# Attention scores as three 64-row products on alternating row halves, in a two-layer encoder of three head groups

## The chip, the core and the metric

The kernel runs on one core of a Trainium2 chip. The metric is the device time of one execution in microseconds. The core has a matrix engine (TensorE; the profile shows its products as PE and the loads of its stationary operands as PEld), VectorE (DVE), ScalarE (ACT), GpSimd (POOL) and a DMA queue that SyncE (SP) issues.

## The reference

Each of two layers normalises x (1024 tokens of 1024 numbers), projects it, and lets three groups of heads work on the result: an mLSTM group, an HGRN2 group and a differential-attention group. Their gated outputs are projected back and added to x. The change touches the attention group, which has four heads. Each head is a pair of query heads and a pair of key heads of 64 numbers, and one value head of 128:

```python
def differential_attention(q, k, v, lam, positions):
    q = rope_partial(q, positions) * (Dq ** -0.5)
    k = rope_partial(k, positions)
    def block(qi):                       # 128 queries against all 1024 keys
        s = jnp.einsum("bqnd,bknd->bnqk", qi, k).astype(jnp.float32)
        p = jax.nn.softmax(s, axis=-1).reshape(B, Hh, 2, Q_BLOCK, S)
        w = p[:, :, 0] - lam * p[:, :, 1]
        return jnp.einsum("bhqk,bkhv->bqhv", w.astype(v.dtype), v)
```

The rotary embedding turns the first 16 of the 64 numbers of a query or key.

## The kernel before

All arrays are float32. Where TensorE is to take a product fast, an operand a is split into a high part in the type fp32r (rounded by an ACT copy) and a low part (the rest, a DVE or GpSimd subtraction), and three products, high by high, high by low and low by high, are summed in PSUM. The input projections are made so (`proj_token`, line 308, and `proj_channel`, line 295: 24 products in one PSUM tile), and the output projection too (line 1058).

**The attention scores** use another form of the split. A head's 64 numbers fill half of the 128 rows of the array, so `evqk` (line 958) writes each 64-number head twice side by side, four heads of 2 x 64 for a tile of 128 tokens. `qk_half` (line 918) rotates both copies (lines 925 to 931) and transposes each doubled head, four tiles of 128 tokens to a PSUM tile (line 936): 16 transposes for 512 tokens. ACT copies the transposed head into fp32r (lines 938 and 941). For a query head, DVE then overwrites rows 64 to 127 with the rest (line 939), so that `Q1` holds the high part above the low part. For a key head all 128 rows are kept as `KH`, which is the high part twice, and `KL`, the low part twice (line 942). A product of `Q1` with `KH` over 128 rows is then high by high plus low by high, and one with `KL` the two other terms.

For each of the four heads (`hd`), each of eight tiles of 128 queries (`qt`) and both query heads of the pair (`n`), two halves of 512 keys (`kb`) take two products each (lines 991 and 992) into one PSUM tile of 1024 columns, `ps_s2`, of which there are two buffers. DVE takes the maximum (line 994) and scales it (995), ACT the exponential and its sum (998). Then the two heads' exponentials are combined on DVE (1003 to 1007), transposed on TensorE (1012), copied out of PSUM by ACT and DVE (1014 and 1016), multiplied with the values (1019), and squared and gated (1021 and 1022). `o_post` (line 901) normalises and transposes a finished head.

**What sets the order.** While head `hd` is worked on, the input projections of head `hd` + 1 are written into the same loop as a generator (`a_proj`, line 944), one piece for each query tile: two tiles of tokens, 48 products of 256 columns. Head 3 has no next head; there the output projection (line 1050 on), which follows in the program, is available. The instruction order on each engine isn't that of the text: the program is built with `schedule_with_timeline_sim=True`, by which a planner lets the program run in a simulation and gives each engine, whenever it is free there, the instruction that stands first in the text among those whose operands and buffers are ready. The order so found is fixed in the program, and each engine then works through it strictly.

Of the kernel before, what the change touches and what calls it, by code (L numbers as in the profile page):

```python
# [9 lines left out]
F32 = mybir.dt.float32  # L10
F32R = mybir.dt.float32r
I32 = mybir.dt.int32
U8 = mybir.dt.uint8
AF = mybir.ActivationFunctionType
ALU = mybir.AluOpType
AX = mybir.AxisListType

P = 128
D = 1024
S = 1024  # L20
# [10 lines left out]
QK = 64  # L31
DMIX = 2048
EPS = 1e-6
HALF = 8
# [56 lines left out]
def trunk(ctx, tc, x_in, positions, w_in, w_out, pvec, rvec, out, dbg=None):  # L91
    nc = tc.nc
# [10 lines left out]
    def ps_mx(name):  # L103
        return pp.tile([P, 512], F32, tag="mx", name=name)

    def ps_s2(name):
        return pp.tile([P, 1024], F32, tag="s2", name=name)
# [12 lines left out]
    ident = cp.tile([P, P], F32, name="ident")  # L120
# [226 lines left out]
    for l in range(DEPTH):  # L347
# [6 lines left out]
        mu_d = dr.tile([8, S], F32, name=f"mu_{l}")  # L354
        mpl_d = dr.tile([16, 8], F32, name=f"mpl_{l}")

        # ------------------------------------------------------------ input norm
        h = []
        if l:
            npool = ExitStack()  # L360
# [1 line left out]
        for half in range(2):  # L362
# [5 lines left out]
            for t4 in range(4):  # L368
                tt = half * 4 + t4
# [14 lines left out]
            for k in range(8):  # L384
                ps = ps_mx(f"hT{l}{half}{k}")
# [6 lines left out]
        npool.close()  # L392
        hpool = ExitStack()
        gp = hpool.enter_context(tc.tile_pool(name=f"hg{l}", bufs=1))
        # ------------------------------------------------------------ mLSTM: conv, q/k/v, gates
        mpool = ExitStack()
        m1 = mpool.enter_context(tc.tile_pool(name=f"mg{l}", bufs=1))
        G = []
        gates = m1.tile([P, NT, 16], F32, name=f"gates{l}")
        nc.vector.tensor_copy(gates, bgate[:, l].unsqueeze(1).broadcast_to([P, NT, 16]))  # L400
        with tc.tile_pool(name=f"ma{l}", bufs=2) as ma:
# [38 lines left out]
            for i in range(3):  # L440
                parts = load_win(l, ("xm", i)) if l or i else xm0
                for jj in range(2):
# [9 lines left out]
                    for k in (0, 1, 3, 4):  # L452
                        d = k - 2
# [8 lines left out]
                    for src, rhs, dd, nm in ((xc, WA[j], xct_d, "a"), (xm, BV[j], v_d, "v")):  # L462
                        tk = ma.tile([P, NT, P], F32, tag="tk", name=f"tk{nm}{l}{j}", bufs=1)
                        for t0 in range(0, NT, 4):
                            ps = ps_s2(f"tk{nm}{l}{j}{t0}")
# [29 lines left out]
        with tc.tile_pool(name=f"mb{l}", bufs=1) as mB:  # L495
# [27 lines left out]
            for d in range(2):  # L523
                rows = []
                for nm, src in (("i", igt), ("f", lgf)):
                    rt = mB.tile([4, S], F32, tag="gr" + nm, name=f"gr{nm}{l}{d}", bufs=2)
                    for half in range(2):
                        ps = ps_mx(f"gr{nm}{l}{d}{half}")
# [12 lines left out]
                for c in order:  # L541
                    sl = slice(c * P, (c + 1) * P)
# [10 lines left out]
                for i, (src, dst) in enumerate(((ir, a_tok), (br, b_tok), (mu, m_tok))):  # L553
                    ps = ps_mx(f"gt{l}{d}{i}")
# [13 lines left out]
                nc.scalar.activation(t, t, AF.Exp)  # L568
            nc.scalar.activation(flr, flr, AF.Exp, scale=-1.0)

        # ------------------------------------------------------------ mLSTM: chunk recurrence
        with tc.tile_pool(name=f"mc{l}", bufs=1) as mp:
            for hd in range(MH):
                pr_, hh_ = divmod(hd, 2)
# [12 lines left out]
                q = mp.tile([P, 2, S], F32, tag="m8", name=f"q{l}{hd}", bufs=2)  # L587
                for i, g in enumerate((G[jA], G[jC][:, hh_])):
                    for half in range(2):
                        sl = slice(half * 512, (half + 1) * 512)  # L590
                        ps = ps_mx(f"q{l}{hd}{i}{half}")
# [3 lines left out]
                for half in range(2):  # L595
                    ps = ps_mx(f"qk{l}{hd}{half}")
                    for c4 in range(4):
                        c = half * 4 + c4
                        sl = slice(c * P, (c + 1) * P)
# [21 lines left out]
                for i in range(NT):  # L621
                    for d in range(2):
                        c = i if d == 0 else NT - 1 - i
                        C = Cs[d]
                        sl = slice(c * P, (c + 1) * P)
                        pn = ps_mx(f"num{l}{hd}{d}{c}")
                        nc.tensor.matmul(pn[:, :MD + 1], W[(d, c)], vt[:, c], start=True, stop=True)
                        n = mp.tile([P, MD + 1], F32, name=f"n{l}{hd}{d}{c}", tag="n", bufs=2)
# [28 lines left out]
                nc.sync.dma_start(hs_d[hd], hsum)  # L657
        mpool.close()

        # ------------------------------------------------------------ HGRN2  # L660
        def slab(name, tag, bufs=None):
            return gp.tile([P, S], F32, tag=tag, name=f"{name}{l}", bufs=bufs or 1)

# [174 lines left out]
            nc.scalar.activation(yo, ps, AF.Copy, scale=hgs[:, l, hd:hd + 1])  # L838
            nc.sync.dma_start(yT[6 + hd], yo)

        # ------------------------------------------------------------ mLSTM: output gates
        md = hpool.enter_context(tc.tile_pool(name=f"md{l}", bufs=1))

        mo = {}
# [51 lines left out]
            {"i": hgrn_iz, "r": hgrn_rest, "o": mlstm_om, "z": mlstm_zm}[step[0]](int(step[1]))  # L896
        hpool.close()

        # ------------------------------------------------------------ attention
        with tc.tile_pool(name=f"at{l}", bufs=2) as ap, tc.tile_pool(name=f"aw{l}", bufs=1) as aw:  # L900
            def o_post(hd, gt, ss, r):
                rstd(ss, r, P)
# [10 lines left out]
                    nc.scalar.activation(yo[:, half * 512:(half + 1) * 512], ps, AF.Copy, scale=ags[:, l, hd:hd + 1])  # L913
                nc.sync.dma_start(yT[12 + hd], yo)

            sets = [ap.tile([P, 3, 2, S], F32R, name=f"qks{l}0", bufs=1), None]

            def qk_half(hd, half, qk):
                Q1, KH, KL = (sets[hd % 2][:, i] for i in range(3))
                cs = cosb[:, half * 4:half * 4 + 4].unsqueeze(2).broadcast_to([P, 4, 4, HALF])  # L920
                sn = sinb[:, half * 4:half * 4 + 4].unsqueeze(2).broadcast_to([P, 4, 4, HALF])
                x1 = qk[:, :, :, 0, 0:HALF]
                x2 = qk[:, :, :, 0, HALF:2 * HALF]
                tmp = [ap.tile([P, 4, 4, HALF], F32, tag=f"rt{i}", name=f"rt{i}{l}{hd}{half}", bufs=1) for i in range(4)]
                nc.vector.tensor_tensor(tmp[0], x1, cs, op=ALU.mult)
                nc.vector.tensor_tensor(tmp[1], x2, sn, op=ALU.mult)
                nc.vector.tensor_tensor(tmp[2], x2, cs, op=ALU.mult)
                nc.vector.tensor_tensor(tmp[3], x1, sn, op=ALU.mult)
                for dup in range(2):
                    nc.vector.tensor_sub(qk[:, :, :, dup, 0:HALF], tmp[0], tmp[1])  # L930
                    nc.vector.tensor_add(qk[:, :, :, dup, HALF:2 * HALF], tmp[2], tmp[3])
                sl = slice(half * 512, (half + 1) * 512)
                for n in range(4):
                    ps = ps_mx(f"qkT{l}{hd}{n}{half}")
                    for t in range(4):
                        nc.tensor.transpose(ps[:, t * P:(t + 1) * P], qk[:, t, n].rearrange("p a d -> p (a d)"), ident)
                    if n < 2:
                        nc.scalar.activation(Q1[:, n, sl], ps, AF.Copy)
                        nc.vector.tensor_tensor(Q1[64:, n, sl], ps[64:], Q1[64:, n, sl].bitcast(F32), op=ALU.subtract)
                    else:  # L940
                        nc.scalar.activation(KH[:, n - 2, sl], ps, AF.Copy)
                        nc.vector.tensor_tensor(KL[:, n - 2, sl], ps, KH[:, n - 2, sl].bitcast(F32), op=ALU.subtract)

            def a_proj(hd, v, gt):
                if hd == 1:
                    sets[1] = aw.tile([P, 3, 2, S], F32R, name=f"qks{l}1", bufs=1)
                pqk = load_win(l, ("aqk", hd))
                pvz = load_win(l, ("avz", hd))

                def evv(ps, tt):  # L950
                    nc.scalar.activation(v[:, tt], ps[:, :P], AF.Copy)
                    nc.scalar.activation(gt[:, tt], ps[:, P:], AF.Tanh, scale=0.5)
                    nc.vector.scalar_tensor_tensor(gt[:, tt], gt[:, tt], 1.0, ps[:, P:], op0=ALU.add, op1=ALU.mult)  # L953
                for half in range(2):
                    qk = ap.tile([P, 4, 4, 2, QK], F32, tag="qk", name=f"qk{l}{hd}{half}", bufs=1)

                    def evqk(ps, tt, qk=qk):
                        nc.scalar.activation(qk[:, tt % 4],
                                             ps.rearrange("p (n d) -> p n d", n=4).unsqueeze(2).broadcast_to([P, 4, 2, QK]), AF.Copy)
                    for t4 in (0, 2):  # L960
                        proj_token(pqk, 2 * P, h, evqk, f"aqk{l}{hd}", [half * 4 + t4, half * 4 + t4 + 1])
                        if t4 == 2:
                            qk_half(hd, half, qk)
                        yield
                    for t4 in (0, 2):
                        proj_token(pvz, 2 * P, h, evv, f"avz{l}{hd}", [half * 4 + t4, half * 4 + t4 + 1])
                        yield
# [9 lines left out]
                pass  # L977
            for hd in range(AH):
                v, gt = vg[hd]
                Q1, KH, KL = (sets[hd % 2][:, i] for i in range(3))  # L980
                nxt = start(hd + 1) if hd + 1 < AH else None
                ss = aw.tile([P, NT], F32, tag="ass", name=f"ass{l}{hd}", bufs=2)
                r = aw.tile([P, NT], F32, tag="ar", name=f"ar{l}{hd}", bufs=2)
                for qt in range(NT):
                    qs = slice(qt * P, (qt + 1) * P)
                    ex, ls = [], []
                    for n in range(2):
                        ps = ps_s2(f"S{l}{hd}{qt}{n}")
                        for kb in range(2):
                            kb_s = slice(kb * 512, (kb + 1) * 512)  # L990
                            nc.tensor.matmul(ps[:, kb_s], Q1[:, n, qs], KH[:, n, kb_s], start=True, stop=False)
                            nc.tensor.matmul(ps[:, kb_s], Q1[:, n, qs], KL[:, n, kb_s], start=False, stop=True)  # L992
                        mx = aw.tile([P, 1], F32, tag="mx", name=f"mx{l}{hd}{qt}{n}", bufs=4)
                        nc.vector.tensor_reduce(mx, ps, axis=AX.X, op=ALU.max)  # L994
                        nc.vector.tensor_scalar_mul(mx, mx, -(QK ** -0.5))  # L995
                        e = aw.tile([P, S], F32, tag="e", name=f"e{l}{hd}{qt}{n}", bufs=4)
                        ls_ = aw.tile([P, 1], F32, tag="ls", name=f"ls{l}{hd}{qt}{n}", bufs=4)
                        nc.scalar.activation(e, ps, AF.Exp, scale=QK ** -0.5, bias=mx, accum_out=ls_)  # L998
                        ex.append(e)
                        ls.append(ls_)  # L1000
# [8 lines left out]
                    for kb in range(2):  # L1009
                        ps = ps_mx(f"wT{l}{hd}{qt}{kb}")  # L1010
# [17 lines left out]
                pend = (hd, gt, ss, r)  # L1028
            o_post(*pend)

        # ------------------------------------------------------------ output projection
        xs = []
        for half in range(2):
            xt = big_tile([P, 4, D], F32, f"xo{l}{half}")
            for t4 in range(4):
                tt = half * 4 + t4
                nc.sync.dma_start(xt[:, t4], x_d[tt] if l else x_in[tt * P:(tt + 1) * P, :])
            xs.append(xt)
        for jp in (3, 4, 5, 0, 1, 2, 6, 7):
# [3 lines left out]
            for j in range(2):  # L1043
                for half in range(2):
                    sl = slice(half * 512, (half + 1) * 512)
# [4 lines left out]
            for tt in range(NT):  # L1050
                ts = slice(tt * P, (tt + 1) * P)
                for nb in range(2):
                    ps = (ps_pj if nb == 0 or jp in OP_PJ else ps_mx)(f"op{l}{jp}{tt}{nb}")
                    i = 0
# [102 lines left out]
```

## Time and profile before

| what | value |
|---|---|
| median of 3 runs | 2910.12 us (2908.21 to 2915.83) |
| span of the profiled execution, its own time | 2911.1 us |
| TensorE products, busy | 2821.4 us (97%), 20004 |
| weight loads, busy | 2467.5 us (85%) |
| VectorE busy | 1847.9 us (63%) |
| ScalarE busy | 1070.5 us (37%) |
| mean granted clock of TensorE | 0.991 |
| attention, first and last score product | 949.6 to 1302 us in layer 0, 2394 to 2746 us in layer 1 |

The profiled execution is known by its span alone. A busy time of TensorE counts a product from its start to its modelled end, and products overlap; the distance between the starts of two products tells what one costs. In a row of the timeline stand the start in us from the span's start, the duration in us, the engine, the line, the operation, the tile written and the tiles read, the shape of the stationary operand (rows*columns), the shape of the moving operand and how many equal instructions are merged in the row. In a row of the grouped view stand the busy time in us, the mean of one in ns, and the idle time before them with what ended it.

### The profile page before, as it was taken

How to read it: one execution, taken by the hardware profiler on the slowest of the kernel's cores; microseconds unless marked ns; L12 is line 12 of the kernel's file. 1: busy time of each engine (PE TensorE's matmuls, PEld its weight loads, DVE VectorE, ACT ScalarE, POOL GpSimd, SP SyncE). 2: the span in 40 equal slices, each digit the busy share in tenths (PEclk: the TensorE clock that was granted, in tenths of full speed). 3: DMA queues.
4: the chain of work that ended last, by engine and by line, in shares of the span. 5: the costliest groups of instructions: out<-in, count | busy, mean ns of one | idle time of the engine just before them, and what ended most of it. 6: DMA issues, size and time to landing. Idle time of an engine off the chain costs nothing. (4 is left out here: it accounts for less than half of the span.)

```text
span 2911.1 us, 49951 instructions
## 1 busy us (share of the span) xinstructions
PE 2821.4 (97%) x20004; PEld 2467.5 (85%) x20004; DVE 1847.9 (63%) x4054; ACT 1070.5 (37%) x2422; POOL 637.3 (22%) x522
## 2 busy tenths in 40 slices
PE   6999999999999999999989999999899999999998
PEld 5888888788888999988879788888898989998886
DVE  6666766575464566696565576666564545767865
ACT  4333323323333445442233423232233324545423
POOL 2122322222123111012211223242121231111112
PEclk9999999999999999999999999999999999999999
DMA  3422212211132001223324211220111221113132
GB/s 119 134 67 67 91 48 73 84 55 45 37 102 95 30 30 37 81 80 93 118 73 131 89 62 52 67 94 30 62 44 44 95 95 30 37 30 109 56 98 104
DMA packets 129864, 210.20 MB, mean 72 GB/s; under 512 B 10832, under 2 KB 60496, under 8 KB 129632
## 3 DMA queue, kind: packets, MB, share of 16 engines
q1 hardware_dynamic: 129632, 207.01, 21.9%
q8 instruction: 157, 2.57, 0.4%
q14 instruction: 75, 0.61, 0.1%
HBM read 156.58 MB, written 50.40 MB: 71 GB/s over the span
## 5 line engine op out<-in xcount | busy, mean ns | idle before, releaser
L137 POOL TENSOR_TENSOR wlo<-wraw,whi 128x512 fp32r<-128x512 f32 x320 | 445.4, 1413 | 1578.5 <-ACT whi L136 1533.6
L1058 PE MATMUL op<-whi,yb 128*128 128x512 f32 x1024 | 333.2, 398 | 0.4 <-DVE xo L1062 0.3
L136 ACT ACTIVATE whi<-wraw 128x512 fp32r<-128x512 f32 x320 | 184.4, 625 | 292.3 <-PE op L1058 85.4
L1062 DVE TENSOR_TENSOR xo<-op,xo 128x512 f32<-128x512 f32 x256 | 174.4, 687 | 96.7 <-PE op L1058 96.6
L308 PE MATMUL pt_hiz<-whi,hh 128*128 128x256 f32 x768 | 225.4, 293 | 6.4 <-DVE hg L674 4.2
L1058 PEld LDWEIGHTS op<-whi,yb 128*128 128x128 f32 x1024 | 192.9, 188 | 45.0 <-DVE xo L1062 1.7
L308 PE MATMUL pt_hiz<-whi,hl 128*128 128x256 f32 x768 | 223.5, 291 | 0.0
L308 PE MATMUL pt_hiz<-wlo,hh 128*128 128x256 f32 x768 | 222.5, 290 | 0.0
L1058 PE MATMUL op<-wlo,yb 128*128 128x512 f32 x512 | 201.9, 394 | 0.0
L639 POOL TENSOR_SCALAR ks<-xcth,wsv 128x192 f32<-128x192 f32 x112 | 111.0, 992 | 388.7 <-PE st L643 345.5
L998 ACT ACTIVATE e<-S,mx 128x1024 f32<-128x1024 f32 x128 | 142.2, 1113 | 142.6 <-DVE mx L995 77.4
L994 DVE TENSOR_REDUCE mx<-S 128x1 f32<-128x1024 f32 x128 | 154.9, 1218 | 36.2 <-PE S L992 35.5
L308 PEld LDWEIGHTS pt_hiz<-whi,hh 128*128 128x128 f32 x768 | 146.4, 191 | 15.1 <-DVE hg L674 5.0
L308 PE MATMUL pt_avz<-whi,hh 128*128 128x256 f32 x512 | 147.8, 289 | 4.4 <-DVE ag L953 4.4
L308 PEld LDWEIGHTS pt_hiz<-wlo,hh 128*128 128x128 f32 x768 | 146.6, 191 | 5.0 <-issue 3.5
L308 PEld LDWEIGHTS pt_hiz<-whi,hl 128*128 128x128 f32 x768 | 146.3, 191 | 3.7 <-issue 2.6
L308 PE MATMUL pt_aqk<-whi,hh 128*128 128x256 f32 x512 | 146.2, 286 | 0.0
L308 PE MATMUL pt_avz<-whi,hl 128*128 128x256 f32 x512 | 145.9, 285 | 0.0
L308 PE MATMUL pt_aqk<-wlo,hh 128*128 128x256 f32 x512 | 145.9, 285 | 0.0
L308 PE MATMUL pt_avz<-wlo,hh 128*128 128x256 f32 x512 | 145.5, 284 | 0.0
L308 PE MATMUL pt_aqk<-whi,hl 128*128 128x256 f32 x512 | 145.2, 284 | 0.0
L1019 PE MATMUL po<-av,wT 128*128 128x128 f32 x1024 | 134.5, 275 | 3.6 <-DVE mx L995 3.4
(358 smaller groups left out, 7560.2 us busy)
## 6 DMA issues: line engine op xcount, KB each, us to landing
wraw<-w_in SPq DMA_DIRECT2D x256, 256.0 KB, 2.8
wraw<-w_out SPq DMA_DIRECT2D x64, 256.0 KB, 2.8
yr<-yT SPq DMA_DIRECT2D x64, 256.0 KB, 2.9
xac<-xcd SPq DMA_DIRECT2D x16, 512.0 KB, 7.2
W<-mu SPq DMA_DIRECT2D x32, 256.0 KB, 3.6
xcd<-xc SPq DMA_DIRECT2D x12, 512.0 KB, 3.0
xct<-tka SPq DMA_DIRECT2D x12, 512.0 KB, 3.4
vd<-tkv SPq DMA_DIRECT2D x12, 512.0 KB, 3.2
```

What stands on the lines that cost most here:

```text
L136: nc.scalar.activation(hi[:, o:o + m], rw[:, :m], AF.Copy)
L137: nc.gpsimd.tensor_sub(lo[:, o:o + m], rw[:, :m], hi[:, o:o + m].bitcast(F32))
L308: nc.tensor.matmul(ps[:, :n], a[:, k, ts], b, start=(i == 0), stop=(i == 23))
L639: nc.gpsimd.tensor_scalar(ks, xct[:, c], wsv[:, d, c, hd:hd + 1], None, op0=ALU.mult)
L994: nc.vector.tensor_reduce(mx, ps, axis=AX.X, op=ALU.max)
L998: nc.scalar.activation(e, ps, AF.Exp, scale=QK ** -0.5, bias=mx, accum_out=ls_)
L1019: nc.tensor.matmul(po[:, :P], wT[:, t * P:(t + 1) * P], v[:, t], start=(t == 0), stop=(t == NT - 1))
L1058: nc.tensor.matmul(ps, a[:, j, ts], b[:, cs_], start=(i == 0), stop=(i == 5))
L1062: nc.vector.tensor_tensor(xv, ps, xv, op=ALU.add)
```

## The change

Queries and keys are no longer doubled. `evqk` copies the projection as it is, the rotation works on one copy, and a transpose takes two heads of 64 numbers at once, so that the query pair of a head lies on rows 0 to 63 and 64 to 127 of one tile, and the key pair likewise. High and low parts are separate tiles: `QH`, `QL`, `KH`, `KL`, 4 x 1024 columns a head instead of 6 x 1024. A score tile takes three products of 64 rows for each half of the keys, and the loop over the two query heads is innermost: the products of `n` = 0 use rows 0 to 63 of the array, those of `n` = 1 rows 64 to 127, and each goes to its own PSUM tile. Both PSUM tiles are asked for ahead of the products. The fourth term, low by low, is no longer computed.

```diff
-            sets = [ap.tile([P, 3, 2, S], F32R, name=f"qks{l}0", bufs=1), None]
+            sets = [ap.tile([P, 4, S], F32R, name=f"qks{l}0", bufs=1), None]
...
-                Q1, KH, KL = (sets[hd % 2][:, i] for i in range(3))
+                qs_ = sets[hd % 2]
...
-                x1 = qk[:, :, :, 0, 0:HALF]
-                x2 = qk[:, :, :, 0, HALF:2 * HALF]
+                x1 = qk[:, :, :, 0:HALF]
+                x2 = qk[:, :, :, HALF:2 * HALF]
...
-                for dup in range(2):
-                    nc.vector.tensor_sub(qk[:, :, :, dup, 0:HALF], tmp[0], tmp[1])
-                    nc.vector.tensor_add(qk[:, :, :, dup, HALF:2 * HALF], tmp[2], tmp[3])
+                nc.vector.tensor_sub(x1, tmp[0], tmp[1])
+                nc.vector.tensor_add(x2, tmp[2], tmp[3])
                 sl = slice(half * 512, (half + 1) * 512)
-                for n in range(4):
-                    ps = ps_mx(f"qkT{l}{hd}{n}{half}")
+                for i in range(2):
+                    ps = ps_mx(f"qkT{l}{hd}{i}{half}")
                     for t in range(4):
-                        nc.tensor.transpose(ps[:, t * P:(t + 1) * P], qk[:, t, n].rearrange("p a d -> p (a d)"), ident)
-                    if n < 2:
-                        nc.scalar.activation(Q1[:, n, sl], ps, AF.Copy)
-                        nc.vector.tensor_tensor(Q1[64:, n, sl], ps[64:], Q1[64:, n, sl].bitcast(F32), op=ALU.subtract)
-                    else:
-                        nc.scalar.activation(KH[:, n - 2, sl], ps, AF.Copy)
-                        nc.vector.tensor_tensor(KL[:, n - 2, sl], ps, KH[:, n - 2, sl].bitcast(F32), op=ALU.subtract)
+                        nc.tensor.transpose(ps[:, t * P:(t + 1) * P],
+                                            qk[:, t, 2 * i:2 * i + 2].rearrange("p a d -> p (a d)"), ident)
+                    nc.scalar.activation(qs_[:, 2 * i, sl], ps, AF.Copy)
+                    nc.vector.tensor_tensor(qs_[:, 2 * i + 1, sl], ps, qs_[:, 2 * i, sl].bitcast(F32), op=ALU.subtract)
...
-                    qk = ap.tile([P, 4, 4, 2, QK], F32, tag="qk", name=f"qk{l}{hd}{half}", bufs=1)
+                    qk = ap.tile([P, 4, 4, QK], F32, tag="qk", name=f"qk{l}{hd}{half}", bufs=1)
...
-                        nc.scalar.activation(qk[:, tt % 4],
-                                             ps.rearrange("p (n d) -> p n d", n=4).unsqueeze(2).broadcast_to([P, 4, 2, QK]), AF.Copy)
+                        nc.scalar.activation(qk[:, tt % 4].rearrange("p n d -> p (n d)"), ps, AF.Copy)
...
-                Q1, KH, KL = (sets[hd % 2][:, i] for i in range(3))
+                QH, QL, KH, KL = (sets[hd % 2][:, i] for i in range(4))
...
+                    sp = [ps_s2(f"S{l}{hd}{qt}{n}") for n in range(2)]
+                    for kb in range(2):
+                        kb_s = slice(kb * 512, (kb + 1) * 512)
+                        for i, (qa, ka) in enumerate(((QH, KH), (QH, KL), (QL, KH))):
+                            for n in range(2):
+                                rs_ = slice(64 * n, 64 * n + 64)
+                                nc.tensor.matmul(sp[n][:, kb_s], qa[rs_, qs], ka[rs_, kb_s], start=(i == 0), stop=(i == 2))
                     for n in range(2):
-                        ps = ps_s2(f"S{l}{hd}{qt}{n}")
-                        for kb in range(2):
-                            kb_s = slice(kb * 512, (kb + 1) * 512)
-                            nc.tensor.matmul(ps[:, kb_s], Q1[:, n, qs], KH[:, n, kb_s], start=True, stop=False)
-                            nc.tensor.matmul(ps[:, kb_s], Q1[:, n, qs], KL[:, n, kb_s], start=False, stop=True)
+                        ps = sp[n]
                         mx = aw.tile([P, 1], F32, tag="mx", name=f"mx{l}{hd}{qt}{n}", bufs=4)
```

More of the change, by code (lines that the diff above doesn't have):

```diff
@@ L928, in qk_half @@
                 nc.vector.tensor_tensor(tmp[3], x1, sn, op=ALU.mult)
-                for dup in range(2):
-                    nc.vector.tensor_sub(qk[:, :, :, dup, 0:HALF], tmp[0], tmp[1])
-                    nc.vector.tensor_add(qk[:, :, :, dup, HALF:2 * HALF], tmp[2], tmp[3])
+                nc.vector.tensor_sub(x1, tmp[0], tmp[1])
+                nc.vector.tensor_add(x2, tmp[2], tmp[3])
                 sl = slice(half * 512, (half + 1) * 512)
-                for n in range(4):
-                    ps = ps_mx(f"qkT{l}{hd}{n}{half}")
+                for i in range(2):
+                    ps = ps_mx(f"qkT{l}{hd}{i}{half}")
                     for t in range(4):
-                        nc.tensor.transpose(ps[:, t * P:(t + 1) * P], qk[:, t, n].rearrange("p a d -> p (a d)"), ident)
-                    if n < 2:
-                        nc.scalar.activation(Q1[:, n, sl], ps, AF.Copy)
-                        nc.vector.tensor_tensor(Q1[64:, n, sl], ps[64:], Q1[64:, n, sl].bitcast(F32), op=ALU.subtract)
-                    else:
-                        nc.scalar.activation(KH[:, n - 2, sl], ps, AF.Copy)
-                        nc.vector.tensor_tensor(KL[:, n - 2, sl], ps, KH[:, n - 2, sl].bitcast(F32), op=ALU.subtract)
+                        nc.tensor.transpose(ps[:, t * P:(t + 1) * P],
+                                            qk[:, t, 2 * i:2 * i + 2].rearrange("p a d -> p (a d)"), ident)
+                    nc.scalar.activation(qs_[:, 2 * i, sl], ps, AF.Copy)
+                    nc.vector.tensor_tensor(qs_[:, 2 * i + 1, sl], ps, qs_[:, 2 * i, sl].bitcast(F32), op=ALU.subtract)
             def a_proj(hd, v, gt):
                 if hd == 1:
-                    sets[1] = aw.tile([P, 3, 2, S], F32R, name=f"qks{l}1", bufs=1)
+                    sets[1] = aw.tile([P, 4, S], F32R, name=f"qks{l}1", bufs=1)
                 pqk = load_win(l, ("aqk", hd))
```

## The prediction

> **What bounds the kernel now.** I read the page's first part, then the busy time by stretch over the attention of the first layer, then the order of TensorE's work.
>
> ```profile
> span 2911.1 us, 49951 instructions
> PE 2821.4 (97%) x20004; PEld 2467.5 (85%) x20004; DVE 1847.9 (63%) x4054; ACT 1070.5 (37%) x2422; POOL 637.3 (22%) x522
> ```
>
> ```profile
> 940.00:1050.00 110.00, 109.30 (x872) 106.25 (x871) 60.80 (x128) 47.97 (x110) 16.13 (x12) 1.00 0.10 30
> 1050.00:1140.00 90.00, 87.22 (x683) 83.42 (x683) 59.68 (x142) 44.47 (x100) 10.21 (x8) 1.00 0.09 30
> 1140.00:1235.00 95.00, 92.14 (x725) 88.31 (x724) 64.40 (x150) 47.27 (x106) 10.23 (x8) 1.00 0.20 73
> 1235.00:1310.00 75.00, 74.65 (x410) 62.88 (x409) 68.65 (x148) 37.63 (x76) 11.24 (x8) 1.00 0.25 78
> ```
>
> The columns of the second fence are length, PE, PEld, DVE, ACT, POOL (each with its count), clock, DMA share, GB/s. The four stretches are heads 0 to 3, each with the next head's projection or, in head 3, the output projection. PE is occupied for 97 to 99% at clock 1.00; DVE comes near it (68.65 of 75 us) only in head 3, and the output projection that fills PE there can move behind. So what counts is **the distance between the starts of TensorE instructions**: a microsecond of PE queue time taken out or put in moves the end by about that, in attention as elsewhere.
>
> **The change part by part.** First the two pieces of PE work that it touches. One row each of the grouped view, with the exponential that waits for the scores, then PE's timeline with a run of eight score products and a group of four transposes.
>
> ```profile
> L991 PE MATMUL S<-qks 128*128 128x512 f32 x256 | 102.8, 401 | 0.0
> L992 PE MATMUL S<-qks 128*128 128x512 f32 x256 | 102.5, 400 | 0.0
> L998 ACT ACTIVATE e<-S,mx 128x1024 f32<-128x1024 f32 x128 | 142.2, 1113 | 142.6 <-DVE mx L995 77.4
> L936 PE MATMUL qkT<-ident,qk 128*128 128x128 f32 x256 | 37.7, 274 | 2.8 <-DVE qk L931 1.4 <-ACT ayo L913 1.4
> ```
>
> ```profile
> 1003.82 0.40 PE L991 MATMUL S<-qks 128*128 128x512 f32 x1
> ...
> 1005.67 0.28 PE L308 MATMUL pt_avz<-whi,hh 128*128 128x256 f32 x1
> 1005.79 0.28 PE L308 MATMUL pt_avz<-wlo,hh 128*128 128x256 f32 x1
> ...
> 1006.39 0.28 PE L308 MATMUL pt_avz<-whi,hh 128*128 128x256 f32 x1
> 1006.50 0.60 PE L936 MATMUL qkT<-ident,qk 128*128 128x128 f32 x4
> 1006.86 0.36 PE L308 MATMUL pt_avz<-wlo,hh 128*128 128x256 f32 x1
> 1007.06 0.28 PE L308 MATMUL pt_avz<-whi,hl 128*128 128x256 f32 x1
> ```
>
> **Transposes.** Of 256 (64 groups of four) half go. From 1006.39 to 1007.06 is 0.67 us where two steps of a projection without the group take 2 x 0.12: a group costs 0.43 us. 32 x 0.43 = **13.9 us less**. This is the surest term. With them go 32 ACT copies, 32 DVE subtractions, 32 DVE rotations and half of each copy of `qk`; I price these at nothing, since PE's work covers them (DVE at 55 to 68% and ACT at 44 to 50% in heads 0 to 2). No DMA changes.
>
> **Score products, paired.** Eight take 1005.67 - 1003.82 = 1.85 us, 0.231 each, 118 us over 64 query tiles. Twelve products of 64 rows take six such steps where the two halves run at once, 1.39 us: 0.464 less per query tile. Where the halves don't meet, twelve steps: 0.924 more. The trace has no row halves, but column halves in alternation:
>
> ```profile
> 264.19 0.22 PE L753 MATMUL lv<-qp,ks 128*64 128x64 f32 x1
> 264.20 0.22 PE L755 MATMUL lv<-qp,ks 128*64 128x64 f32 x1
> 264.25 0.22 PE L753 MATMUL lv<-qp,ks 128*64 128x64 f32 x1
> 264.26 0.22 PE L755 MATMUL lv<-qp,ks 128*64 128x64 f32 x1
> ```
>
> Partners start 0.01 us apart and the pair recurs every 0.06, with both weight loads hidden. I take 0.231 per pair of row halves; the other end is 0.462, no overlap at all. The Trainium skill ("TensorE: Matmul & The Clock Gate", Measured speedup vs the span model) puts four row tiles of 32 rows at 3.07 times one instead of 4, which speaks against a full pair; by that share, as an estimate, a pair would take 0.231 x 4/3.07 = 0.301 us and 40 paired query tiles 17 us more than I count, 2955 us in all; no run here shows row tiles side by side.
>
> **Where do the halves meet?** The planner puts on each engine whatever is ready first in program order, and the scores of the next query tile serve as filler. I followed all 512 score products through PE's order: for 64 query tiles there are 128 separate runs of them, of lengths 1 to 8. Two kinds matter, here in heads 2 and 3:
>
> ```profile
> 1149.74 0.40 PE L991 MATMUL S<-qks 128*128 128x512 f32 x1
> 1149.98 0.28 PE L308 MATMUL pt_aqk<-whi,hl 128*128 128x256 f32 x1
> ```
>
> ```profile
> 1256.91 0.60 PE L1012 MATMUL wT<-ident,e 128*128 128x128 f32 x4
> 1257.27 0.48 PE L991 MATMUL S<-qks 128*128 128x512 f32 x1
> 1257.59 0.40 PE L992 MATMUL S<-qks 128*128 128x512 f32 x1
> ...
> 1258.05 0.39 PE L992 MATMUL S<-qks 128*128 128x512 f32 x1
> 1258.28 0.39 PE L1058 MATMUL op<-whi,yb 128*128 128x512 f32 x1
> ...
> 1261.06 0.39 PE L991 MATMUL S<-qks 128*128 128x512 f32 x1
> ```
>
> The first is a lone product, a projection step right behind it. The second is four of one query head, other work, four of the other: a head's scores start when the exponentials of the tile before have freed its one of two PSUM buffers (`s2`, two buffers), and these come free at different times. The new order alternates in the program text, but it needs **both** buffers; where the planner sees one free, the products of that head are ready alone and go first, six in a row on one half. In all of head 3 (8 query tiles a layer) and in the first two of heads 1 and 2 the runs have this shape: 12 a layer, 24 in all. I count 40 query tiles paired, 24 alone: -40 x 0.464 + 24 x 0.924 = **3.6 us more**. Bounds: all paired -29.7, none +59.1. If the planner instead kept the order, PE would stand at the second product until the later exponential is done; I give that no price, since runs of eight show both buffers free by then, but it could reach the 1.11 us of one exponential (L998) per query tile, 71 us.
>
> **Changes of shape.** Today every product of attention is 128 by 128. The row halves are another shape, and the trace shows what PE does at a change, with column halves and with a 4-row stationary:
>
> ```profile
> 262.67 0.49 PE L642 MATMUL st<-vth,ks 128*128 128x193 f32 x2
> 263.09 0.54 PE L643 MATMUL st<-vth,ks 128*64 128x193 f32 x2
> 263.56 0.43 PE L627 MATMUL num<-vth,W 128*128 128x193 f32 x1
> 263.83 0.33 PE L627 MATMUL num<-vth,W 128*128 128x193 f32 x1
> ```
>
> ```profile
> 194.28 0.39 PE L295 MATMUL pc_hfb<-hh,wlo 128*128 128x512 f32 x1
> 194.60 0.66 PE L556 MATMUL gt<-ident,gri 4*128 4x4 f32 x8
> ...
> 195.69 0.50 PE L295 MATMUL pc_hfb<-hh,whi 128*128 128x512 f32 x1
> ```
>
> Into the 4-row shape the step is 0.32 us (194.28 to 194.60) where 512 columns take 0.23 in the run of scores: 0.09 lost. Two L642 of 193 columns stream for 2 x 0.16 us (0.49 for both, 0.33 for one), yet L643 comes after 0.42: 0.10 lost; from the two L643 to L627 it is 0.47, 0.15 lost, of which I count 0.05, half of the 0.10 below, as the first weight load of half the width that nothing hides. Back in the full shape the first product is 0.10 or 0.11 longer (0.43 for 0.33, 0.50 for 0.39), its load in the open. A round trip: 0.09 in, 0.05 for the first half-height load (ends 0, all of it hidden, and 0.10, the full load), 0.09 out, 0.10 reload: 0.33 us. 46 of the 128 runs follow a transpose or an f32 product and pay 0.08 of this already (0.48 for 0.40 at 1257.27), 0.03 on average. So **0.30 us for each run, 128 runs: 38.4 us more**; ends 0.25 and 0.35. Nothing covers it: the queue of PE is what is full. The Trainium skill ("TensorEngine Tiling (Array Packing)", Key Properties) says that a change of tiling mode drains the TensorE while a change of tile does not, which is the rule that speaks against this change. These rows agree for the shapes that they have, and give the price that the page doesn't; where it did not hold for row halves, the sum above would be 38.4 us lower, 2900.
>
> The first head's scores also become complete later (after eleven twelfths of a run, not a half), 0.4 us for VectorE's reduction; projections cover it, and without that cover it would be 64 x 0.4 = 26 us.
>
> **Sum:** -13.9 + 3.6 + 38.4 = +28.1 us on the profiled span of 2911.1, which is 1.0 above the median of the runs (2910.1): **2938 us**, slower by 1%.
>
> **The rivals.** A difference under 0.3% (9 us) can't be told from none.
>
> *Whole runs.* The alternation binds the two heads together, so that each query tile is one run, all paired. -13.9 - 29.7 + 64 x 0.30 = -24.4: **2886 us**, faster. For it speak the runs of eight at 1003.82 and their like; against it the buffers that come free apart, and that the filler gets cut wherever something earlier in the program becomes ready. With everything paired it decides at (13.9 + 29.7)/0.30 = 145 runs: below, the kernel gets faster.
>
> *Paired but cut.* 128 runs as today, all paired: -13.9 - 29.7 + 38.4 = -5.2, **2905 us**, no difference to be told.
>
> *No drain between these shapes.* -13.9 - 29.7 = -43.6: **2867 us**. Against it the 4-row rows above.
>
> *No overlap*, the change doing not what it says: -13.9 + 59.1 + 38.4 = +83.6: **2994 us**. For it: two row halves write the same 128 PSUM partitions, which column halves don't. Against it: they lie in different buffers, and PE runs column halves together.
>
> **How the numbers follow.** Forecast 0.42, whole runs 0.23, paired but cut 0.15, no overlap 0.14, no drain 0.06. The forecast's own range is 2914 (100 runs of 0.25, 16 tiles alone) to 2967 (160 runs of 0.35, 32 alone). The range 2882 to 2980 leaves out no drain and no overlap, 0.2. Faster: 0.23 + 0.06 + 0.03 of paired but cut, 0.32; same: its other 0.12 and 0.02 of the forecast, 0.14; slower: 0.40 + 0.14 = 0.54.
>
> **What would show it.** Transposes: 128 of `qkT`, not 256. Pairs: rows of S with 64*128 that start within 0.02 us of each other, a pair every 0.23; alone: single rows every 0.23, six of one head in a row, above all in head 3. Shape: 0.09 us more before the first S of a run and a first full product that is 0.10 longer after it; some 128 runs. The forecast is wrong if there are near 64 runs, if head 3 shows pairs, or if a pair takes twice 0.23.

## The result and the profile after

The changed kernel takes **2940.71 us** (median of 4 runs, 2938.66 to 2943.31) and the kernel before 2911.94 (4 runs beside it, 2908.21 to 2915.83). The ratio is **1.0098, interval 1.0083 to 1.0112**: slower by 1%. The forecast was 2938. The profiled executions stand at 2936.9 and 2911.1 us, 25.8 us apart, and the working below is done on these two.

The first part of the page of the kernel after, and two rows of its grouped view:

```profile
span 2936.9 us, 50101 instructions
...
PE 2844.4 (97%) x20132; PEld 2446.7 (83%) x20132; DVE 1825.2 (62%) x3990; ACT 1042.3 (35%) x2390; POOL 641.3 (22%) x522
```

```profile
L988 PE MATMUL S<-qks 64*128 64x512 f32 x768 | 145.4, 415 | 0.3 <-ACT e L996 0.2
L935 PE MATMUL qkT<-ident,qk 128*128 128x128 f32 x128 | 19.2, 278 | 1.2 <-DVE qk L930 1.2
```

VectorE and ScalarE do less than before (1825.2 for 1847.9, 1042.3 for 1070.5), the transposes are halved, and TensorE is busy for 23.0 us more in a longer span. Its timeline shows where, with a run of scores in head 1 and one in head 3:

```profile
1056.53 0.28 PE L308 MATMUL pt_avz<-whi,hl 128*128 128x256 f32 x1
1056.74 1.66 PE L988 MATMUL S<-qks 64*128 64x512 f32 x12
1058.33 0.39 PE L308 MATMUL pt_aqk<-whi,hh 128*128 128x256 f32 x1
1058.55 0.28 PE L308 MATMUL pt_aqk<-wlo,hh 128*128 128x256 f32 x1
...
1241.37 1.66 PE L988 MATMUL S<-qks 64*128 64x512 f32 x6
1242.95 0.50 PE L1056 MATMUL op<-whi,yb 128*128 128x512 f32 x1
1243.29 0.39 PE L1056 MATMUL op<-wlo,yb 128*128 128x512 f32 x1
...
1245.92 1.65 PE L988 MATMUL S<-qks 64*128 64x512 f32 x6
```

**Twelve products take 1.59 us in head 1, and six take 1.58 us in head 3.** In the first the halves alternate and run at once; in the second all six are of one half, and the six of the other half come as a run of their own (1245.92). The edges are seen too: 0.21 us from the last projection product to the first score (0.12 between projection products), and 0.22 instead of 0.12 behind the first projection product after the run.

The busy times of layer 0's attention in one stretch, before and after (columns as in the prediction), and what TensorE waited for there, with total, times and longest wait:

```profile
930.00:1285.00 355.00, 348.31 (x2624) 329.26 (x2623) 235.56 (x530) 168.93 (x374) 50.88 (x38) 1.00 0.15 51
```

```profile
930.00:1285.00 355.00, 351.53 (x2669) 315.07 (x2667) 218.41 (x497) 154.16 (x357) 45.31 (x34) 1.00 0.15 51
```

```profile
PE pt_avz L308 <- DVE ag L953: 2.2, 2, 1.1
PE po L1019 <- DVE mx L995: 1.7, 2, 0.9
PE wT L1012 <- DVE ag L1022: 1.0, 2, 0.6
PE qkT L936 <- DVE qk L931: 0.7, 1, 0.7
```

```profile
PE po L1017 <- DVE mx L993: 2.7, 3, 0.9
PE qkT L935 <- DVE qk L930: 0.6, 1, 0.6
```

The first of each pair is before. TensorE stood for 6.7 us before and for 3.5 us after: the change also took waits away, a gain that the prediction did not have.

To add up where the time went I took the distances between the starts of all TensorE instructions in both attentions, from the first product of `pt_aqk` to the last score. "Scores" is the time from entry to exit of all runs of S, beyond the usual step of the product before; "gaps" is what other distances have beyond the usual step of their kind; "rest" is what then remains to the change of the span, and lies in the other stages.

| kernel | span | runs of scores | scores | transposes | gaps | rest |
|---|---|---|---|---|---|---|
| before | 2911.1 | 128 | 118.6 | 27.6 | 27.5 | |
| after | 2936.9 | 110 | +38.6 | -13.8 | -10.2 | +11.2 |
| whole_first | 2926.0 | 82 | +1.7 | -13.8 | +14.6 | +12.4 |
| whole | 2914.5 | 92 | +8.2 | -13.8 | -4.3 | +13.3 |
| one_half_at_a_time | 2974.0 | 118 | +72.1 | -13.8 | -12.5 | +17.1 |
| serial_full_rows | 2957.7 | 118 | +60.4 | -13.8 | -13.6 | +13.6 |
| transposes_alone | 2888.3 | 108 | -0.5 | -13.8 | -12.0 | +3.5 |
| doubled_by_copies | 2901.5 | 148 | +4.2 | -13.8 | -2.5 | +2.5 |

All in us; the last four columns are, from the second row on, differences from before. Whole_first and the kernels below it are the experiments.

### The profile page after: what moved, and what is told of

Read it like the earlier page. It is cut to its first block, busy times and chain, and to the rows that moved or that the text cites. A ratio compares the mean times of both kernels' runs of the same rounds, so it can differ in the third digit from the quotient of the medians.

```text
span 2936.9 us, 50101 instructions
## 1 busy us (share of the span) xinstructions
PE 2844.4 (97%) x20132; PEld 2446.7 (83%) x20132; DVE 1825.2 (62%) x3990; ACT 1042.3 (35%) x2390; POOL 641.3 (22%) x522
## 5 line engine op out<-in xcount | busy, mean ns | idle before, releaser
L988 PE MATMUL S<-qks 64*128 64x512 f32 x768 | 145.4, 415 | 0.3 <-ACT e L996 0.2
L308 PE MATMUL pt_aqk<-whi,hl 128*128 128x256 f32 x512 | 145.4, 284 | 0.0
```

The source lines that it names most:

```text
L308: nc.tensor.matmul(ps[:, :n], a[:, k, ts], b, start=(i == 0), stop=(i == 23))
L988: nc.tensor.matmul(sp[n][:, kb_s], qa[rs_, qs], ka[rs_, kb_s], start=(i == 0), stop=(i == 2))
```

## The experiments

**Score products bound together and put first.** The twelve products of a query tile are chained in order, the first also waits for both exponentials of the tile before, and the planner is told that they are more urgent than anything else.

```diff
+                    with tc.high_priority():
...
-                            for n in range(2):
...
+                                for n in (1, 0):
...
-                                nc.tensor.matmul(sp[n][:, kb_s], ...)
+                                    last = chain(nc.tensor.matmul(sp[n][:, kb_s], ...), last)
+                                    while freed:
+                                        behind(last, freed.pop())
```

> The changed kernel, its twelve score products of a query tile tied to one another in program order on TensorE, the first of them also behind both exponentials of the tile before (so that both PSUM buffers are free), and the planner told to take them ahead of all other work. Planned order: 82 runs of scores instead of 110, every product beside its partner. Theory 1 (the loss is 228 products without a partner and about 0.36 us for each change of shape there and back, 110 of them): 114 steps of 0.231 us less = -26 us, 28 round trips less = -10 us, so about 2940 - 36 = 2904 us, a little below the kernel before. Theory 2 (the loss lies in twelve weight loads and products in place of eight, whatever their order): no gain, 2935 to 2945 us. Theory 3 (row halves that start together still slow each other): the pairs recur every 0.30 us rather than every 0.23, and the time stays above 2915.

It took 2927.45 us, ratio to before 1.0042 (1.0027 to 1.0057). The group of the scores, the stretch of layer 0's attention and its waits:

```profile
L1006 PE MATMUL S<-qks 64*128 64x512 f32 x768 | 111.0, 413 | 0.0
```

```profile
930.00:1285.00 355.00, 345.93 (x2715) 313.76 (x2714) 225.46 (x508) 155.88 (x364) 50.02 (x38) 1.00 0.16 53
```

```profile
PE qkT L949 <- DVE qk L944: 3.8, 4, 1.1
PE po L1038 <- DVE wT L1035: 1.7, 1, 1.7
PE pt_avz L322 <- DVE ag L963: 1.4, 2, 0.7
```

The scores behave as theory 1 says: all 768 products have a partner, there are 82 runs, and their time falls by 36.9 us against the changed kernel (busy 111.0 for 145.4). But the time is 23 us above the 2904 of that theory: TensorE now stands for 9.1 us of this stretch instead of 3.5, and the gaps over both layers grow by 24.8 us. The price of a run comes out again: 384 steps of 0.231 are 88.7 us of the 120.3, and the other 31.6 over 82 runs are **0.385 us each**; in the changed kernel it is (157.2 - 498 x 0.231) / 110 = **0.383**.

**Bound together, without the urgency.** The same without `high_priority`.

> As whole_first, but the planner places the scores by their place in the text, not ahead of everything. Planned order: 92 runs, 748 of 768 products beside their partner. The traces so far: score stage 0.231 us a step plus 0.385 a run. Theory 1: 388 steps and 92 runs are 89.6 + 35.4 = 125 us of PE time against 157 in the changed kernel, and the 28 us of stalls that whole_first had in attention fall back to the changed kernel's 8, so about 2940 - 32 = 2908 us, level with the kernel before (2905 to 2915). If the stalls of whole_first come from binding the scores together and not from placing them first, it is as slow as whole_first, 2925 us or more.

2917.68 us, ratio 1.0011 (1.0002 to 1.0021): 23 us below the changed kernel, and a difference from before that is too small to count.

```profile
L1005 PE MATMUL S<-qks 64*128 64x512 f32 x768 | 116.0, 415 | 0.8 <-ACT e L1016 0.8
```

```profile
930.00:1285.00 355.00, 349.80 (x2711) 315.99 (x2711) 223.13 (x506) 156.66 (x363) 47.27 (x37) 1.00 0.18 55
```

The two kernels differ by the urgency alone. It saves 6.5 us of scores and costs 18.9 us of gaps: so most of the gaps of the first kernel come from putting the scores ahead of other work; by its first wait, `qkT` behind `qk`, that is work which VectorE and TensorE have to do for the next head. The binding by itself gives a time that is 10 us above the 2908 of theory 1. That theory started from the changed kernel, and against it the scores fall by 30.4 us and not 32, the gaps grow by 5.9 and the rest by 2.1, which the theory had at nothing: 9.6 us.

**One half after the other.** Six products of one query head, then six of the other, chained.

```diff
-                    for kb in range(2):
...
+                    for n in range(2):
+                        rs_ = slice(64 * n, 64 * n + 64)
+                        for kb in range(2):
+                            for i, (qa, ka) in enumerate(((QH, KH), (QH, KL), (QL, KH))):
+                                last = chain(nc.tensor.matmul(sp[n][:, kb_s], qa[rs_, qs], ka[rs_, kb_s], ...), last)
```

> The changed kernel with the six products of one query head first and then the six of the other, tied in program order, so that hardly any product has a partner (100 of 768 at the joints). Planned order: 118 runs. Theory 1: from the changed kernel (2940) the 540 products that had partners there become 270 - 50 = 220 steps of 0.231 us more = +51 us, 8 round trips more = +3, about 2994 us. If the row halves brought nothing by running together (no overlap in what the trace shows as common starts), no change, 2940 to 2945 us.

2975.99 us, ratio 1.022 (1.0204 to 1.0237). It was slower than the changed kernel by 35 us, as a loss of pairs should be, but 18 us less than expected. The reason lies in this run:

```profile
983.32 0.28 PE L315 MATMUL pt_aqk<-whi,hl 128*128 128x256 f32 x1
983.53 2.24 PE L996 MATMUL S<-qks 64*128 64x512 f32 x12
985.70 0.39 PE L315 MATMUL pt_aqk<-whi,hh 128*128 128x256 f32 x1
```

From the start of the run to the next product are 2.17 us, less than twelve steps of 0.231 (2.77): part of the twelve ran in pairs although they stand six and six in the program. More on this in the last section.

**The same order with 128 rows.** The products of the kernel above take all 128 rows, so that their shape is that of everything else. They then sum over both query heads, whose scores are not separated.

```diff
-                                last = chain(nc.tensor.matmul(sp[n][:, kb_s], qa[rs_, qs], ka[rs_, kb_s], ...), last)
+                                last = chain(nc.tensor.matmul(sp[n][:, kb_s], qa[:, qs], ka[:, kb_s], ...), last)
```

> As one_half_at_a_time, in the same planned order of all instructions, but each score product takes all 128 rows, so that TensorE never changes its shape; the scores of the two query heads then are not separated, which is left out. Twelve products in turn, no pairs. Theory 1: 2912 - 14 (transposes) + 64 x 4 x 0.231 = +59, so about 2957 us, and about 118 x 0.36 = 42 us less than one_half_at_a_time, less some 12 us for the 50 pairs that exist at its joints: 30 to 42 us between them. Theory 2 (changes of shape cost nothing): the same as one_half_at_a_time or above it.

2961.25 us, ratio 1.0164 (1.0149 to 1.0179).

```profile
979.75 0.28 PE L315 MATMUL pt_aqk<-whi,hl 128*128 128x256 f32 x1
979.86 2.92 PE L995 MATMUL S<-qks 128*128 128x512 f32 x12
982.62 0.28 PE L315 MATMUL pt_aqk<-whi,hh 128*128 128x256 f32 x1
982.73 0.28 PE L315 MATMUL pt_aqk<-wlo,hh 128*128 128x256 f32 x1
```

The trace has the same instructions in the same order as that of the kernel above, with 118 runs of the same lengths, and these don't pay: entry 0.11, twelve steps in 2.76 us, exit and next product 0.11 apart. What exceeds 768 steps of 0.231 is 1.6 us, 0.014 for a run. So **the price belongs to the 64-row shape**, not to the cutting of the scores into runs. The time is 14.7 us below that of the kernel above, where 30 to 42 were expected. In the scores it is 11.7 us by the table: the runs save 118 x 0.383 = 45.2 us and pay 1.6, and some 138 steps (31.9 us) are lost that the row halves shared there, many more than the 50 pairs counted on (the last section counts the steps).

**The transposes alone.** The queries and keys of the changed kernel, and four products of 128 rows for a query head, as many as before. Here too the scores of the two query heads are not separated.

```diff
...
+                    for n in range(2):
+                        for kb in range(2):
...
+                            nc.tensor.matmul(sp[n][:, kb_s], QH[:, qs], KH[:, kb_s], start=True, stop=False)
+                            nc.tensor.matmul(sp[n][:, kb_s], QH[:, qs], KL[:, kb_s], start=False, stop=True)
```

> One part alone: queries and keys no longer doubled, half the transposes, but the scores as two products of all 128 rows each, eight for a query tile as in the kernel before (the scores of the two query heads are not separated, which is left out). Theory 1: 32 groups of transposes at 0.43 us less, 2912 - 14 = 2898 us. If copies and subtractions behind the transposes had covered them: no change, 2907 to 2915 us.

2886.86 us, ratio 0.9911 (0.9896 to 0.9926): 11 us less than expected.

```profile
930.00:1285.00 355.00, 353.18 (x2646) 333.86 (x2645) 231.08 (x523) 161.64 (x371) 53.26 (x40) 1.00 0.18 57
```

```profile
PE qkT L935 <- ACT ayo L913: 0.7, 2, 0.3
PE qkT L935 <- DVE qk L930: 0.6, 1, 0.6
```

The transposes give the 13.8 us that were counted. Beside them the gaps fall by 12.0 us: of the 6.7 us that TensorE stood before, 1.8 are left, and the waits for `ag` and `mx` are gone.

**Doubled by copies.** Half the transposes, but the doubled arrays of the kernel before: ACT and DVE write each half of `Q1`, `KH` and `KL` from the transposed pair, and the scores are those of before.

```diff
...
+                    for n, (at, to) in enumerate(((up, dn), (dn, up))):
+                        if i == 0:
+                            nc.scalar.activation(Q1[at, n, sl], ps[at], AF.Copy)
+                            nc.vector.tensor_tensor(Q1[to, n, sl], ps[at], Q1[at, n, sl].bitcast(F32), op=ALU.subtract)
+                        else:
+                            for o in (at, to):
+                                nc.scalar.activation(KH[o, n, sl], ps[at], AF.Copy)
+                                nc.vector.tensor_tensor(KL[o, n, sl], ps[at], KH[at, n, sl].bitcast(F32), op=ALU.subtract)
...
```

> Half the transposes without row halves: queries and keys are transposed undoubled, two heads at once, and the doubling and the high and low parts are made behind the transpose by ACT copies and DVE subtractions that write the other 64 partitions (six of each for 512 tokens in place of four). The scores stay as before, eight products of 128 rows, no change of shape. Theory 1 (transposes and the stalls behind them are what undoubling saves, shapes and lone products what it costs): 2912 - 14 = 2898 us from the transposes alone, down to 2888 if the stalls at a head's start go too as in transposes_alone; 2905 or more if the extra copies and subtractions hold the transposes' PSUM buffers and PE waits for them.

**2900.66 us, ratio 0.9956 (0.9942 to 0.9970): faster than both kernels.**

```profile
930.00:1285.00 355.00, 346.51 (x2586) 326.13 (x2586) 243.97 (x542) 176.47 (x396) 50.04 (x38) 1.00 0.18 57
```

```profile
PE S L993 <- ACT qks L944: 2.2, 1, 2.2
PE po L1021 <- DVE mx L997: 1.7, 2, 0.9
PE pt_avz L308 <- DVE mx L997: 1.5, 2, 0.8
PE wT L1014 <- ACT wT L1016: 1.4, 2, 0.7
```

The waits are back: 8.5 us of the stretch, and 9.5 us more of gaps than with the transposes alone. VectorE works 13 us more there and ScalarE 15 us more. The two kernels have the same transposes and as many products; what differs is the copies, and that transposes_alone asks for both score buffers at once. One wait, the longest, is for a copy itself (`qks`, 2.2 us); the others are for other work of VectorE and ScalarE. So it is likely that the work of the two engines on queries and keys, which I had priced at nothing, is what TensorE waits for at these places. How much of it comes from the copies, and how much from the two buffers, was not taken apart.

**The boundary of the layers.** 11.2 us of the change lie outside the two attentions. Between the last product of the output projection and the first transposes of the next layer (before, then after; PE, and ScalarE's fourth square sum behind the projection):

```profile
1457.85 0.39 PE L1058 MATMUL op<-whi,yb 128*128 128x512 f32 x1
1458.08 1.03 PE L387 MATMUL hT<-ident,xt 128*128 128x128 f32 x8
```

```profile
1447.92 1.06 ACT L341 ACTIVATE sq<-xo 128x1024 f32<-128x1024 f32 x1 [1.64 <-DVE xo L1062]
```

```profile
1465.41 0.39 PE L1056 MATMUL op<-whi,yb 128*128 128x512 f32 x1
1468.85 0.69 PE L387 MATMUL hT<-ident,xt 128*128 128x128 f32 x2 [3.05 <-DVE xt L383]
```

```profile
1461.04 1.06 ACT L341 ACTIVATE sq<-xo 128x1024 f32<-128x1024 f32 x1 [3.02 <-DVE xo L1060]
```

TensorE goes on after 0.23 us before and after 3.44 us now, waiting for the normalised tokens. One experiment marks the normalisations (that behind the last layer too) as most urgent in the changed kernel, a second does so in the kernel doubled by copies, whose boundary has no such wait:

```diff
+            with tc.high_priority():
+                r = norm_stats(np_, srcs, f"{l}{half}")
...
```

> The changed kernel, with the normalisation behind each layer (its squares, its reciprocal roots and its multiplications) marked as more urgent for the planner than everything else. In the changed kernel TensorE stands for 3.4 us between the last product of the output projection of layer 0 (1465.41) and the first transposes of layer 1 (1468.85), 0.2 us before the change; the transposes then take 35.3 us for 31.8, and 13.9 us lie behind the last product of all for 9.9. Theory 1: these 11 us come from the order that the planner gives VectorE there, the multiplications of the first tokens behind the last sum of the projection, and not from the row halves. Then the wait falls to under 1 us and the transposes to about 32 us; with the end unchanged the time is some 7 us shorter than the changed kernel's 2940.7, 2934, and with the end as before the change, 2930. Theory 2: TensorE reaches the boundary with something else late (the sums of squares on ScalarE), so that the order changes nothing: 2940 and 3.4 us of wait.

> The same edit of the urgency in the kernel that doubles queries and keys by copies (2900.7 us), where the wait at the layer boundary is 0.2 us and 9.6 us lie behind the last product already. Theory 1 (the boundary is a matter of VectorE's order alone): the edit has nothing to gain here, 2900 within 4 us. Theory 2 (something else is late there): also 2900. A control: if it gets faster or slower by more than 6 us, the urgency moves something other than the boundary, and the result of the other kernel can't be read as the boundary's.

2940.94 us (ratio 1.0095, 1.0081 to 1.0108) and 2901.54 us (0.9963, 0.9949 to 0.9976): neither moved. In the first the wait is the same:

```profile
1468.56 0.40 PE L1057 MATMUL op<-whi,yb 128*128 128x512 f32 x1
1472.00 0.69 PE L388 MATMUL hT<-ident,xt 128*128 128x128 f32 x2 [3.04 <-DVE xt L384]
```

But the edit did not try what it was meant to try. In both traces TensorE, VectorE, ScalarE and GpSimd do the same instructions in the same order as in the same kernel without the urgency, so theory 1 of that experiment, VectorE's order, is not decided. The rows above tell how the two boundaries differ: the fourth square sum, the last that the first half of the tokens needs, starts 9.9 us ahead of the last product before, and 4.4 us ahead of it after, since it waits for a sum `xo` that the projection finished later (3.02 us of idle ahead of it). Eight additions of the projection follow its start before, and four after: the output projection ends its tiles in another order. In both kernels VectorE puts such additions between the steps of the normalisation; in the changed one three of them take 2.4 of the 4.8 us from the first step (1462.26) to the multiplication (1467.02), so an order without them may shorten the wait. That the other order of the tiles comes from the place where the longer scores left the projection is likely, since the kernels with twelve products for a query tile have this wait (3.4 or 3.5 us in all six) and those with eight don't (0.2 to 0.5); it was not tried.

## Why the prediction was right, step by step

The time was forecast at +28.1 us on the span and came out at +25.8. The mechanisms it names are there, but that the sum comes out so close is luck: two items of ten microseconds each that it had at nothing, one up and one down, and smaller errors of both signs cancel.

- **Transposes, -13.9:** -13.8, in every kernel that has half of them. The group of four costs what the prediction read from one place of the timeline.
- **Price of the copies, nothing:** gaps fell by 10.2 us. The step failed where it covered ScalarE's and VectorE's work by the average over a head; TensorE was waiting for them in a few places, 6.7 us in all in the stretch of layer 0 quoted above. Transposes_alone (-12.0) and doubled_by_copies (-2.5) point to the copies, but the asking for both buffers changed between them too, so that the cause of this item is not fully shown.
- **Pairs at 0.231:** right. Twelve alternating products take 1.59 us with both edges. The estimate of 0.301 that the prediction drew from the Trainium skill ("TensorE: Matmul & The Clock Gate", Measured speedup vs the span model) does not hold for two halves of 64 rows.
- **24 tiles alone, 40 paired (+3.6):** the mechanism held, the count was high. Of 768 products 228 had no partner, 19 tiles' worth, so the term is 19 x 0.924 - 45 x 0.464 = -3.3. Seven of the eight tiles of head 3 in each layer are six and six, as read from the freeing of the two buffers; the first is paired, which the last line of the prediction had as a sign against it. In heads 1 and 2 the first two tiles, which were to be alone, are paired, and others are alone (the fifth of both, the third of head 2 and the second of head 0): that reading was wrong, and only the number came near. In six runs the sixes of the two halves stand side by side and share four steps; these are counted as pairs.
- **128 runs:** 110.
- **0.30 us for a run:** the term that was mis-sized; it is 0.383. In (0.21 for 0.12), out (0.32 to the next full product instead of 0.23) and reload (0.22 for 0.12) are the 0.09, 0.09 and 0.10 of the prediction. The first load of half the height is not half hidden: the first step of a run is 0.337 us where the others are 0.231, 0.11 and not 0.05, at the upper of the two ends given. The rest is what runs behind transposes had paid already, less than I took off. In all 110 x 0.383 = 42.1 for the 38.4 forecast. Serial_full_rows, whose runs pay 0.014, shows that it is the shape; the Trainium skill ("TensorEngine Tiling (Array Packing)", Key Properties) has the rule without the price, and the trace agrees with it.
- **The sum outside attention, nothing:** +11.2. The work that the longer scores pushed behind attention runs 3.6 us less densely there, the boundary costs 3.2 and the transposes behind it 3.5, and 13.9 us instead of 9.9 lie behind the last product; other stages give 3.1 back. The 4.0 us more behind the last product need not come from the longer scores: transposes_alone, with eight products for a query tile, has 13.4 us there. What causes the 11.2 stays open.

The errors against the forecast: pairing -6.9, fewer runs 18 x 0.30 = -5.4, price of a run 110 x 0.083 = +9.1, gaps -10.2, outside +11.2, transposes +0.1 make -2.1 of the -2.3 us.

**The rivals.** No overlap and no drain are excluded by the rows of the two runs, and *paired but cut* by the 228 products without a partner. *Whole runs* named the right lever but not all that it pulls: with all or nearly all products paired (768 and 748) and 82 to 92 runs the kernel is at 2918 to 2927 us and not at 2886, because runs are more than 64, each costs 0.385, and what is gained in the scores turns into waits and into the end of the layer. By the decision point of that rival, worked with 0.385, (13.9 + 29.7) / 0.385 = 113 runs would still pay; 92 did not, since 13.3 us were lost outside.

## What to carry to other kernels

Count how often a row-tiled product meets a full one in the queue of TensorE: here a visit cost 0.385 us, as much as 1.7 products of 512 columns, while a whole query tile of six pairs saved 0.464 against full rows, so that a tile cut into two visits already loses. Alternation in the text is worth only as much of it as the planner keeps: here it held where both output buffers came free together. And an engine that is busy for two thirds of a stretch (VectorE, 235.56 of 355 us before) can still be what the bound engine waits for; look at the waits at the seams before pricing its work at nothing.

## What the runs showed that was not expected

**TensorE pairs row halves that are not neighbours in its queue.** The quoted row of the run at 983.53, in the kernel that issues six products of one half and then six of the other, merges twelve products; their single starts in the trace lie at 0, 0.337, 0.573, 0.580, 0.801, 0.915, 1.034, 1.150, 1.265, 1.383, 1.619 and 1.843 us from the first. The fourth start is 7 ns behind the third and its product is as long as a first one (0.493 us, like the first with 0.497; the others 0.383 to 0.394), and the semaphore of the first six is set by the ninth start, not by the sixth. So the seventh product of the queue began with the third, and ran beside the rest of the first half; the whole took 2.17 us where the full-row kernel with the same order took 2.76. Over all 118 runs of that kernel (190.7 - 118 x 0.383) / 0.231 gives 630 steps for 768 products. In the changed kernel the run at 980.60 has the same pattern. The Trainium skill ("TensorE: Matmul & The Clock Gate", The mechanism) says that products start and end strictly in the order of the program; these starts differ from that. In all 50 runs of the one-half kernel that hold both halves, the first product of the second half starts within 0.02 us of the one four places ahead of it in the program (the third of six in 30 runs, the second of five in 2, the first of four in 14); where only two or three stand ahead, it starts with the first of them (4 runs). Why it is four stays open.
